# A hybrid decoder layer on one Trainium2 core: expert gathers spread more thinly over the early stages, a later transpose step, and a shorter decode of top-k positions

## The chip, the cores and the metric

The kernel is one launch on one core of one Trainium2 chip. The metric is device time in microseconds (us). Three runs of the kernel before took 3212.78, 3213.16 and 3213.87 us; the median is 3213.16 us. One further execution was profiled: it took 3213.83 us, of which the profile's span covers 3212.0 us.

## The reference, cut to what matters

One layer over 1024 tokens of width 1024, batch 1:

```
h = rms_norm(x);  proj = h @ w_in                    # q, k, v of 4 attention heads; q, k, v, o, i, f of 4 mLSTM heads
da_out = differential attention(q, k, v)             # causal, ALiBi, 4 heads of 2 x 64
ml_out = chunkwise mLSTM(conv(q), conv(k), v, i, f)  # 4 heads of 128
x = x + concat(da_out, ml_out) @ w_out
q = rms_norm(x) @ w_query                            # 8 heads x 2 halves x 128
s = q . sub_keys                                     # 128 keys per half
sv, si = top_k(s, 16)                                # per half
top_s, pos = top_k(sv0[:, None] + sv1[None, :], 16)  # 16 of the 256 pairs
eidx = 128 * si0[row of pos] + si1[column of pos]    # 8 x 16 experts per token
x = x + sum_k softmax(top_s)_k * gelu(h2 . expert_u[eidx_k]) * expert_v[eidx_k]
x = x + sigmoid(rms_norm(x) @ w_ple_gate) * (p @ w_ple_proj)
out = rms_norm(x)
```

There are 16384 experts, each a row of 1024 floats in `expert_u` and in `expert_v`. `h2` is the normalised input of this step.

## The kernel before, in words

**Stages.** The 1024 tokens are two parts of 512 (T); a part is four tiles of 128 tokens. `front(0)` and `front(1)` compute, for one part each, the projections, attention, mLSTM, the output projection, and the retrieval scores with their top 16 per half. Of the eight tiles, the first three (NS = 3, the sparse tiles) fetch their chosen expert rows by gather; the other five (640 tokens) go through all experts densely: `dense_up` multiplies them with all of `expert_u` in 128 blocks `j`, applies GELU and stores the result, and builds the gate matrix that says which token takes which expert; `dense_down` multiplies with all of `expert_v` in 128 blocks, four at a time. `tail` does the last gate, projection and norm for each of the eight tiles, in the order 4, 0, 5, 6, 7, 1, 3, 2. Matmuls run in a split form: each fp32 operand is a high and a low part (`hi` by ACT, `lo` by DVE), and three products replace one.

**The gathered steps.** For the three sparse tiles, `sparse` is a generator of 400 steps: 24 units of 16 experts, and one more unit's worth of steps that finishes the last. A step has a u half and a v half. The u half (line 803) gathers one row of `expert_u` per token (512 KB, an indirect DMA issued by POOL, line 788) and takes its dot product with `h2` on DVE (line 804). The v half, 16 steps later, gathers the row of `expert_v` and adds it, scaled, to the running sum `ya` on DVE (line 822). The first 16 steps have only the u half, the last 16 only the v half. Ahead of them in the same generator stand 14 steps of `topk2` for the first two tiles. When the last v half of a tile is done, the sum is stored to DRAM (line 826), and `tail` reads it back (line 1086).

**What paces them.** `pump(x)` (line 210) adds x to a running sum and emits one step for each whole unit; it is called from `project` (line 289, F_RATE[0], 29 times in `front(1)`), at the eight loads of output weights (line 609, F_RATE[2]), at the 16 query projections (lines 658 and 669, F_RATE[1]), at each block j of `dense_up` (line 940: the first UP_RATE value below block UP_RATE[2], then the second), four times DOWN_RATE per group of four blocks of `dense_down`, and TAIL_RATE twice per tile of `tail`, until the steps are used up. In `front(0)` nothing is pumped (the rates are multiplied by `part`). The program's instructions are put in order at build time by a planner that gives each emitted instruction a priority in order of emission; what `pump` emits comes 800 places later (LAG), so gathers fill gaps that the planner sees on DVE. The DVE half of a step also stands behind the last weight split before it (`behind`, line 203). On the chip each engine takes its instructions strictly in that order.

**Buffers.** Gathered rows land in a ring: `ru` and `rv` have NR = 4 buffers each from `front(1)` to the end of `dense_up`, six each in `dense_down`, two each from group FLUSH of `dense_down` on and in `tail`. In `front` most [128, 512] tiles come from one ring named `t2` with 8 buffers: q and k after projection (lines 370, 379), their copies to both 64-row halves (`doubled`, line 257, four per head in part 0 and six in part 1), and attention and mLSTM temporaries.

**Order of the steps in `front`.** `attention(h)` is a generator of six steps (five for its four query tiles, the sixth with the norm `ro` of the outputs and their transposes, lines 444 to 449), `ml_inputs(h)` of four (each one projection), `mlstm(h)` of four (the fourth with the transposes of its outputs, line 558), `qkv(h)` of three (each one projection). The loop over heads (lines 570 to 580) calls them in turn.

**Decoding.** A top-k position `pos` in the 50 candidate pairs is taken apart in `topk2b` (lines 751 to 762): row a starts at OFFS[a] (0, 16, 24, 29, 33, 36, 38, 40, 42, 43, ... 49) and has COUNTS[a] columns (16, 8, 5, 4, 3, 2, 2, 2, then eight rows of one). For each a from 1 to 15 two instructions add the row's index to `i0`, and two subtract the length of the row before from `bb`, which ends as the column. This runs for four groups of two tiles: one in `front(1)`, three in the first 42 blocks of `dense_up`.

Of the kernel before, what the change touches and what calls it, by code (L numbers as in the profile page):

```python
# [8 lines left out]
F32 = mybir.dt.float32  # L9
F32R = mybir.dt.float32r  # L10
BF16 = mybir.dt.bfloat16
# [4 lines left out]
OP = mybir.AluOpType  # L16
# [3 lines left out]
P = 128  # L20
D = 1024
S = 1024
T = 512
# [5 lines left out]
K = 16  # L29
# [5 lines left out]
COUNTS = [K // (a + 1) for a in range(K)]  # L35
OFFS = [sum(COUNTS[:a]) for a in range(K)]
# [11 lines left out]
LAG = 800  # L48
FLUSH = 108
NPRE = 4  # L50
NR = 4
NR2 = 2
NRD = 6
RD = 2
# [8 lines left out]
T2 = 8  # L63
# [3 lines left out]
TORD = [4, 0, 5, 6, 7, 1, 3, 2]  # L67
TAIL_RATE = 8.0
TKEYS = [(0, q) for q in range(4)] + [(0, -1), (1, -1)] + [(1, q) for q in range(4)]
F_RATE = (2.4, 1.6, 2.0)  # L70
UP_RATE = (1.0, 1.2, 56)
DOWN_RATE = 1.05


# [1 line left out]
def layer(ctx, tc, x, xT, pT, gcols, grows, win, convw, convb, gbias, lams, wout, wq, subk,  # L76
# [3 lines left out]
    def pool(name, bufs=1, **k):  # L80
        if k.get("space") != bass.MemoryType.DRAM:
            k["reuse_waits"] = "tile"
        return tc.tile_pool(name=name, bufs=bufs, **k)

    v, sc, pe, gp, sy = nc.vector, nc.scalar, nc.tensor, nc.gpsimd, nc.sync
# [132 lines left out]
    def front(part, ptk):  # L218
        t0 = part * NT
        with ExitStack() as c1:  # L220
# [4 lines left out]
            with pool(f"pa{part}", bufs=1) as pa:  # L225
# [29 lines left out]
                        sc.activation(kab[halves[c], 1 - c, 1, n * T:(n + 1) * T], kb[halves[c]], AF.Copy)  # L255

                def doubled(src, c):
                    d = pa.tile([P, T], F32, name="t2", bufs=T2)
                    for half in halves:
                        sy.dma_start(d[half], src[halves[c]])  # L260
                    return d
# [44 lines left out]
                for i in range(NT):  # L306
                    v.scalar_tensor_tensor(gt[:, i, :], gps[:, i, 0:8], r1[:, i:i + 1], gb, op0=OP.mult,
                                           op1=OP.add)
# [58 lines left out]

                def qkv(h):
                    ps = project(h * 7 + 0)
                    qT = pa.tile([P, T], F32, name="t2", bufs=T2)  # L370
                    v.scalar_tensor_tensor(qT, ps, DA_SCALE, rb, op0=OP.mult, op1=OP.mult)
                    queries(qT, h)
                    vv = pa.tile([P, S // P, P], F32, name="vv", bufs=1)
                    if part:
                        keys(kt_s[h], 0)
                        sy.dma_start(vv[:, :NT, :], v_s[h])
                    yield
                    ps = project(h * 7 + 1)
                    kT = pa.tile([P, T], F32, name="t2", bufs=T2)
                    v.tensor_tensor(kT, ps, rb, op=OP.mult)  # L380
                    if part < NPART - 1:
                        sy.dma_start(kt_s[h], kT)
                    keys(kT, part)
                    yield
                    ps = project(h * 7 + 2)
                    by_tile(vv[:, t0:t0 + NT, :], token_major(ps), lambda i: r1[:, i:i + 1])
                    if part < NPART - 1:
                        sy.dma_start(v_s[h], vv[:, :NT, :])
                    st["qkv", h] = (qT, kT, vv)
                    yield  # L390
# [171 lines left out]
                def step(*gens):  # L562
                    for g in gens:
                        if g is not None:
                            next(g, None)
# [3 lines left out]
                cell = None  # L569
                for h in range(H):  # L570
                    att, inputs = attention(h), ml_inputs(h)
                    step(att, cell)
                    for _ in range(4):
                        step(inputs, att)
                    step(att)
                    cell = mlstm(h)
                    nxt = qkv(h + 1) if h + 1 < H else None
                    for _ in range(3):
                        step(cell, nxt)
                step(cell)  # L580

                mh = act.tile([P, DC, T], F32R, name="ahi")
# [125 lines left out]
    def topk2b(part, pt_, tgs):  # L708
        sv, sfa = fcs["sv", part]
        t0 = part * NT  # L710
        i0a, i1a = sel_i[part]
        gsa = gsm[part]
        TG = 2
        G = TG * PH
        for tg in tgs:
            def grp(a):
                return a[:, tg:tg + TG, :].rearrange("p t (h k) -> p (t h) k", k=K)

            svf = sv[:, tg:tg + TG].rearrange("p t h c k -> p (t h) c k")
            sif = sfa[:, tg:tg + TG].rearrange("p t h c k -> p (t h) c k")  # L720
            cand = pt_.tile([P, G, NCAND], F32, name="cand")
            for a in range(8):
                n = COUNTS[a]
                behind(v.tensor_tensor(cand[:, :, OFFS[a]:OFFS[a] + n], svf[:, :, 1, 0:n],
                                       svf[:, :, 0, a:a + 1].to_broadcast([P, G, n]), op=OP.add))
            behind(v.tensor_tensor(cand[:, :, OFFS[8]:], svf[:, :, 0, 8:],
                                   svf[:, :, 1, 0:1].to_broadcast([P, G, 8]), op=OP.add))
            yield True
            ts = pt_.tile([P, G, K], F32, name="ts")
            pu_ = pt_.tile([P, G, K], U32, name="pu_")  # L730
            for j in range(G):
                wk = pt_.tile([P, NCAND], F32, name="wk2", bufs=2)
                v.max(out=ts[:, j, 0:8], in_=cand[:, j, :])
                v.max_index(out=pu_[:, j, 0:8], in_max=ts[:, j, 0:8], in_values=cand[:, j, :])
                v.match_replace(out=wk, in_to_replace=ts[:, j, 0:8], in_values=cand[:, j, :],
                                imm_value=NEG)
                v.max(out=ts[:, j, 8:16], in_=wk)
                v.max_index(out=pu_[:, j, 8:16], in_max=ts[:, j, 8:16], in_values=wk)
                if j % 4 == 3:
                    yield True  # L740
            pos = pt_.tile([P, G, K], BF16, name="pos")
            v.tensor_copy(pos, pu_)
            dl = pt_.tile([P, G, 2, K], BF16, name="dl")
            v.tensor_copy(dl[:, :, :, 0:1], sif[:, :, :, 0:1])
            v.tensor_tensor(dl[:, :, :, 1:], sif[:, :, :, 1:], sif[:, :, :, :K - 1], op=OP.subtract)
            i0, i1 = grp(i0a), grp(i1a)
            bb = pt_.tile([P, G, K], BF16, name="bb")
            v.tensor_copy(i0, dl[:, :, 0, 0:1].to_broadcast([P, G, K]))
            v.tensor_copy(i1, dl[:, :, 1, 0:1].to_broadcast([P, G, K]))
            v.tensor_copy(bb, pos)  # L750
            for a in range(1, K):
                tmp = pt_.tile([P, G, K], BF16, name="tmp", bufs=1)
                v.scalar_tensor_tensor(tmp, pos, float(OFFS[a]),
                                       dl[:, :, 0, a:a + 1].to_broadcast([P, G, K]),
                                       op0=OP.is_ge, op1=OP.mult)
                v.tensor_tensor(i0, i0, tmp, op=OP.add)
                tmp = pt_.tile([P, G, K], BF16, name="tmp", bufs=1)
                v.tensor_scalar(tmp, pos, float(OFFS[a]), float(COUNTS[a - 1]), op0=OP.is_ge,
                                op1=OP.mult)
                v.tensor_tensor(bb, bb, tmp, op=OP.subtract)  # L760
                if a % 3 == 0:
                    yield True
            for b in range(1, K):
                tmp = pt_.tile([P, G, K], BF16, name="tmp", bufs=1)
                v.scalar_tensor_tensor(tmp, bb, float(b),
                                       dl[:, :, 1, b:b + 1].to_broadcast([P, G, K]),
                                       op0=OP.is_ge, op1=OP.mult)
                v.tensor_tensor(i1, i1, tmp, op=OP.add)
                if b % 4 == 0:
                    yield True  # L770
            if t0 + tg < NS:
                v.scalar_tensor_tensor(grp(eidx[part]), i0, 128.0, i1, op0=OP.mult, op1=OP.add)
            g_ = grp(gsa)
            gs = pt_.tile([P, G], F32, name="gs")
            v.tensor_tensor(g_, ts, ts[:, :, 0:1].to_broadcast([P, G, K]), op=OP.subtract)
            sc.activation(g_, g_, AF.Exp)
            v.tensor_reduce(out=gs, in_=g_, axis=AX.X, op=OP.add)
            gr = pt_.tile([P, G], F32, name="gr")
            v.reciprocal(gr, gs)
            v.tensor_tensor(g_, g_, gr[:, :, None].to_broadcast([P, G, K]), op=OP.mult)  # L780
            yield True

    ring, stored = {}, set()
# [365 lines left out]
    rstk = ctx.enter_context(ExitStack())  # L1149
    ptk = rstk.enter_context(pool("ptk", side="right"))  # L1150
    fc = fstk.enter_context(pool("fc"))
    front(0, ptk)
    ring["pool"] = rstk.enter_context(pool("rg", side="right"))
    ring["bufs"] = NR
    pumped["gen"] = chain(lambda: topk2(0, ptk, [0]), lambda: sparse(range(NS), rs))
    front(1, ptk)
    fstk.close()
    dense_up(ptk)
    stk.close()
    yap = ctx.enter_context(pool("yap"))  # L1160
# [93 lines left out]
```

## Time and profile before

| | us |
|---|---|
| median of three runs | 3213.16 |
| profiled execution | 3213.83 |
| its span | 3212.0 |
| PE (matmul) busy in the span | 2954.8 (92%) |
| DVE busy | 2521.5 (79%) |
| ACT busy | 1160.2 (36%) |
| POOL busy | 1013.0 (32%) |

Stages in the span, by when their first and last instructions run: `front(0)` to about 460 us, `front(1)` to about 1060, `dense_up` to about 2110, `dense_down` to about 3057, `tail` to the end.

PE is the tensor engine, DVE the vector engine, ACT the scalar engine, POOL the engine that issues gathers, SP the queue of most other DMAs. "L804" is line 804 of the kernel. An arrow such as "ru<-ru,sh" reads output<-inputs by the program's tile names. In square brackets stands how long the engine sat idle before an instruction and what ended the wait.

### The profile page before, as it was taken

What the parts mean: (1) busy time and instruction counts of PE and PEld (TensorE: products, weight loads), DVE (VectorE), ACT (ScalarE), POOL (GpSimd) and SP (SyncE); (2) the same over time, 40 slices, a digit from 0 to 9 for tenths busy, and PEclk for the clock granted to TensorE, in tenths of its full rate; (3) what the DMA queues carried; (4) which work ended last, traced back from release to release, by engine and by line L of the source; (5) the groups of instructions that cost most, each with busy time, mean ns of one, the idle gap of its engine ahead of it and who ended that gap; (6) DMA issues with size and microseconds to landing.
All of it is one profiled execution on the core that took longest, in us unless ns stands there. A gap on an engine that the chain in (4) does not pass through costs nothing.

```text
span 3212.0 us, 44687 instructions
## 1 busy us (share of the span) xinstructions
PE 2954.8 (92%) x16367; PEld 2601.1 (81%) x16367; DVE 2521.5 (79%) x5381; ACT 1160.2 (36%) x1994; POOL 1013.0 (32%) x786
## 2 busy tenths in 40 slices
PE   7998889887579799999999999988989999999987
PEld 6776767676467799999999999977878888887866
DVE  5564689888889999978766667557878888888786
ACT  5664335554322232245343433322222222222233
POOL 0000000344541544412433334343333444442330
PEclk9998989998789899999999999989999999999999
DMA  5333433678874788876888878899989999998762
GB/s 163 96 107 108 143 120 95 232 234 274 323 264 147 290 317 313 284 262 244 329 314 299 293 278 311 313 343 343 327 316 337 334 334 331 334 327 286 265 209 92
DMA packets 317148, 829.53 MB, mean 258 GB/s; under 512 B 26240, under 2 KB 115200, under 8 KB 314368
## 3 DMA queue, kind: packets, MB, share of 16 engines
q0 software_dynamic: 112608, 410.04, 36.2%
q1 hardware_dynamic: 185888, 374.68, 33.8%
q10 hardware_dynamic: 18432, 41.95, 3.5%
q8 instruction: 128, 2.10, 0.3%
q14 instruction: 92, 0.75, 0.1%
HBM read 715.95 MB, written 102.24 MB: 255 GB/s over the span
## 4 chain that ended last, share of the span: by engine, by line
PE 53%; DVE 19%; issue 14%; DMA 8%; POOL 4%; ACT 2%; SPq 0%; POOLq 0%; DVEq 0%; ACTq 0%
PE A L143 16%; PE mm L143 10%; PE keep L143 6%; DVE ya L822 3%; PE S L143 3%; DVE ru L804 2%; DMA rv<-in_ev,eidx 2%; PE Y L135 2%; PE Y L134 2%; PE Y L136 2%; DMA raw<-in_vr 2%; POOL rv L788 2%; PE pg L894 2%; PE pg L895 2%; DVE tlo L842 2%
## 5 line engine op out<-in xcount | busy, mean ns | idle before, releaser
L788 POOL DMA_INDIRECT ru<-in_eu,eidx x384 | 507.5, 1321 | 1201.8 <-DVE ru L804 845.1
L788 POOL DMA_INDIRECT rv<-in_ev,eidx x384 | 497.5, 1296 | 442.6 <-DVE ya L822 300.7
L842 DVE TENSOR_TENSOR tlo<-raw,thi 128x1024 fp32r<-128x1024 f32 x256 | 312.9, 1222 | 299.1 <-issue 168.5
L822 DVE SCALAR_TENSOR_TENSOR ya<-rv,cf,ya 128x1024 f32<-128x1024 f32 x384 | 492.8, 1283 | 40.3 <-DMA rv<-in_ev,eidx 28.1
L841 ACT ACTIVATE thi<-raw 128x1024 fp32r<-128x1024 f32 x256 | 268.0, 1058 | 683.4 <-PE A L143 380.8
L804 DVE SCALAR_TENSOR_TENSOR ru<-ru,sh 128x1024 f32<-128x1024 f32 x384 | 468.8, 1221 | 20.8 <-DMA ru<-in_eu,eidx 19.6
L143 PE MATMUL A<-ahi,thi 128*128 128x384 f32 x1024 | 348.7, 341 | 4.3 <-ACT ga L954 4.3
L143 PE MATMUL A<-alo,thi 128*128 128x384 f32 x1024 | 346.6, 338 | 0.0
L143 PE MATMUL mm<-ahi,whi 128*128 128x512 f32 (+1 forms) x752 | 299.7, 402 | 22.2 <-ACT ahi L234 12.4
L143 PE MATMUL mm<-alo,whi 128*128 128x512 f32 (+1 forms) x752 | 286.2, 393 | 7.1 <-DVE alo L235 7.1
L134 PE MATMUL Y<-thi,ph 128*128 128x512 f32 x640 | 250.3, 391 | 6.6 <-ACT thi L841 4.8
L143 PE MATMUL A<-xh,thi 128*128 128x256 f32 x1024 | 250.8, 283 | 0.7 <-ACT xh L933 0.7
L143 PE MATMUL A<-xl,thi 128*128 128x256 f32 x1024 | 250.6, 282 | 0.1
L135 PE MATMUL Y<-tlo,ph 128*128 128x512 f32 x640 | 249.8, 390 | 0.5 <-DVE tlo L842 0.5
L136 PE MATMUL Y<-thi,pl 128*128 128x512 f32 x640 | 249.5, 390 | 0.0
L143 PE MATMUL A<-ahi,tlo 128*128 128x384 f32 x1024 | 202.7, 338 | 13.8 <-DVE tlo L842 13.7
L1021 ACT ACTIVATE ph<-aq 128x640 fp32r<-128x640 f32 x128 | 87.5, 729 | 330.8 <-PE Y L135 325.3
L143 PEld LDWEIGHTS A<-ahi,thi 128*128 128x128 f32 x1024 | 195.1, 191 | 4.5 <-ACT ga L954 4.5
L143 PE MATMUL mm<-ahi,wlo 128*128 128x512 f32 (+1 forms) x752 | 193.7, 388 | 5.5 <-DVE wlo L194 5.5
L143 PEld LDWEIGHTS A<-xh,thi 128*128 128x128 f32 x1024 | 195.0, 190 | 1.0 <-ACT xh L933 0.9
L143 PEld LDWEIGHTS A<-xl,thi 128*128 128x128 f32 x1024 | 194.8, 190 | 0.3 <-DVE xl L934 0.3
L143 PEld LDWEIGHTS A<-alo,thi 128*128 128x128 f32 x1024 | 195.0, 190 | 0.0
(462 smaller groups left out, 6160.0 us busy)
## 6 DMA issues: line engine op xcount, KB each, us to landing
raw<-in_ut SPq DMA_DIRECT2D x128, 512.0 KB, 5.9
raw<-in_vr SPq DMA_DIRECT2D x128, 512.0 KB, 5.5
ga_s<-ga ACTq DMA_DIRECT2D x128, 320.0 KB, 5.6
g_s<-st SPq DMA_DIRECT2D x20, 2048.0 KB, 8.3
gq<-g_s SPq DMA_DIRECT2D x32, 1280.0 KB, 10.8
aq<-ga_s SPq DMA_DIRECT2D x32, 1280.0 KB, 8.7
wraw<-in_win SPq DMA_DIRECT2D x58, 512.0 KB, 3.4
wraw<-in_wq SPq DMA_DIRECT2D x32, 512.0 KB, 3.7
```

The costliest lines, as they stand in the source:

```text
L134: pe.matmul(o, lh, rh, start=start, stop=False)
L135: pe.matmul(o, lh, rl, start=False, stop=False)
L136: pe.matmul(o, ll, rh, start=False, stop=stop)
L143: pe.matmul(o, ll if p == "l" else lh, rl if p == "r" else rh, start=start and p == "h", stop=stop and n == last and p == names[-1])
L788: gp.indirect_dma_start(out=b, out_offset=None, in_=table, in_offset=bass.IndirectOffsetOnAxis(ap=eidx[part][:, i, k:k + 1], axis=0))
L804: behind(v.scalar_tensor_tensor(b, b, 1.0, st["h", tl], op0=OP.mult, op1=OP.mult, accum_out=st["d", n][:, j:j + 1]))
L822: op = v.scalar_tensor_tensor(ya, b, st["c", n][:, j:j + 1], ya, op0=OP.mult, op1=OP.add)
L841: sc.activation(hi, raw, AF.Copy)
L842: anchor(v.tensor_sub(lo, raw, hi.bitcast(F32)))
L894: pe.matmul(pg[:, b, :], o0[:, a, :, b], w0[:, a, :, b], start=True, stop=False)
L895: pe.matmul(pg[:, b, :], o0[:, a, :, b], w1[:, a, :, b], start=False, stop=True)
L1021: sc.activation(ph, av, AF.Copy)
```

## The change

- Rates of the gathered steps: F_RATE, UP_RATE.
- The gather ring: 3 buffers each in `front(1)` (NR), a new pool `rgu` with 4 each (NRU) opened for `dense_up`.
- `doubled` takes its copies from a ring `dd` of its own with 2 buffers, and q and k after projection from a ring `qk` with 2; `t2` keeps 8.
- In the loop over heads the fourth step of the head before's mLSTM comes after the first projection of `ml_inputs` (it came before it). The last line calls the attention generator twice; as it has six steps, of which five are taken above, the second call finds it ended.
- Decoding: for a from 9 to 15 nothing is subtracted from `bb`; at a = 8 one instruction sets `bb` to zero where `pos` is at least OFFS[8] = 42. The instructions for `i0` stay.

```diff
-NR = 4
+NR = 3
+NRU = 4
+NDD = 2
-F_RATE = (2.4, 1.6, 2.0)
-UP_RATE = (1.0, 1.2, 56)
+F_RATE = (1.8, 1.3, 1.5)
+UP_RATE = (0.9, 1.45, 40)
...
                 def doubled(src, c):
-                    d = pa.tile([P, T], F32, name="t2", bufs=T2)
+                    d = pa.tile([P, T], F32, name="dd", bufs=NDD)
...
-                    qT = pa.tile([P, T], F32, name="t2", bufs=T2)
+                    qT = pa.tile([P, T], F32, name="qk", bufs=2)
...
-                    kT = pa.tile([P, T], F32, name="t2", bufs=T2)
+                    kT = pa.tile([P, T], F32, name="qk", bufs=2)
...
                     att, inputs = attention(h), ml_inputs(h)
-                    step(att, cell)
-                    for _ in range(4):
+                    step(att)
+                    step(inputs, cell, att)
+                    for _ in range(3):
                         step(inputs, att)
-                    step(att)
                     cell = mlstm(h)
                     nxt = qkv(h + 1) if h + 1 < H else None
-                    for _ in range(3):
-                        step(cell, nxt)
+                    step(att, cell, nxt, cell, nxt, att, cell, nxt)
                 step(cell)
...
-                tmp = pt_.tile([P, G, K], BF16, name="tmp", bufs=1)
-                v.tensor_scalar(tmp, pos, float(OFFS[a]), float(COUNTS[a - 1]), op0=OP.is_ge,
-                                op1=OP.mult)
-                v.tensor_tensor(bb, bb, tmp, op=OP.subtract)
+                if a < 8:
+                    tmp = pt_.tile([P, G, K], BF16, name="tmp", bufs=1)
+                    v.tensor_scalar(tmp, pos, float(OFFS[a]), float(COUNTS[a - 1]), op0=OP.is_ge,
+                                    op1=OP.mult)
+                    v.tensor_tensor(bb, bb, tmp, op=OP.subtract)
+                elif a == 8:
+                    v.scalar_tensor_tensor(bb, pos, float(OFFS[8]), bb, op0=OP.is_lt, op1=OP.mult)
...
-    ring["pool"] = rstk.enter_context(pool("rg", side="right"))
+    fring = ExitStack()
+    ring["pool"] = fring.enter_context(pool("rg", side="right"))
     ring["bufs"] = NR
...
     fstk.close()
+    fring.close()
+    ring["pool"] = rstk.enter_context(pool("rgu", side="right"))
+    ring["bufs"] = NRU
     dense_up(ptk)
```

## Rows read from the trace of the kernel before

**Rows 1.** Busy time of each engine by stretch: PE, PEld, DVE, ACT, POOL, PE clock, DMA share, GB/s.

```profile
680.00:772.00 92.00, 72.30 (x375) 59.28 (x376) 82.67 (x158) 45.56 (x104) 46.15 (x38) 0.87 0.80 272
...
1043.00:1080.00 37.00, 19.24 (x88) 16.25 (x88) 37.00 (x163) 5.14 (x8) 18.93 (x14) 0.72 0.68 229
...
1500.00:2097.00 597.00, 596.72 (x4233) 592.83 (x4232) 413.44 (x454) 232.61 (x321) 236.37 (x176) 1.00 0.85 304
...
2125.00:2250.00 125.00, 102.21 (x434) 83.66 (x434) 89.55 (x114) 28.34 (x37) 51.10 (x42) 0.90 1.02 359
...
2400.00:2650.00 250.00, 250.00 (x1105) 207.01 (x1104) 212.40 (x270) 60.69 (x75) 100.75 (x76) 1.00 0.96 334
...
3060.00:3156.00 96.00, 84.49 (x360) 66.36 (x361) 75.38 (x192) 35.93 (x68) 27.78 (x23) 0.95 0.61 198
```

**Rows 2.** Line 804 on DVE by stretch: busy (two records per u half), clock, DMA.

```profile
460.00:870.00 410.00, 74.74 (x122) 0.86 0.68 228
...
717.00:749.00 32.00, 13.42 (x22) 0.79 0.98 368
870.00:940.00 70.00, 18.43 (x30) 0.88 0.85 317
1043.00:1080.00 37.00, 8.59 (x14) 0.72 0.68 229
```

**Rows 3.** Line 822 on DVE by stretch: busy (one record per v half).

```profile
717.00:749.00 32.00, 14.06 (x11) 0.79 0.98 368
...
1500.00:2097.00 597.00, 113.10 (x88) 1.00 0.85 304
3060.00:3156.00 96.00, 26.94 (x21) 0.95 0.61 198
```

**Rows 4.** DVE in order of time: start, duration, line, operation, tiles.

```profile
721.22 0.20 DVE L116 TENSOR_SCALAR ro_m<-oss 128x4 f32<-128x4 f32 x1
...
730.16 1.27 DVE L822 SCALAR_TENSOR_TENSOR ya<-rv,cf,ya 128x1024 f32<-128x1024 f32 x1
731.36 0.15 DVE L125 SCALAR_TENSOR_TENSOR ro_u<-ro_h,ro_u 128x4 f32<-128x4 f32 x1
731.43 1.22 DVE L804 SCALAR_TENSOR_TENSOR ru<-ru,sh 128x1024 f32<-128x1024 f32 x1
...
732.57 0.15 DVE L123 TENSOR_TENSOR ro_h<-ro_u 128x4 f32<-128x4 f32 x1
...
735.26 0.16 DVE L125 SCALAR_TENSOR_TENSOR ro_u<-ro_h,ro_u 128x4 f32<-128x4 f32 x1
```

**Rows 5.** PE in order of time, the transposes of lines 448 and 558.

```profile
735.91 1.06 PE L448 MATMUL tr<-ident,t 128*128 128x128 f32 x3 [12.17 <-ACT t L364]
...
589.90 0.33 PE L558 MATMUL tr<-ident,t 128*128 128x128 f32 x1 [0.26 <-ACT t L364]
```

**Rows 6.** Who waited for whom: PE from 870 to 940, then 1030 to 1085.

```profile
PE tr L635 <- DVE dg L631: 17.3, 1, 17.3
...
PE A L143 <- DVE tlo L842: 13.7, 1, 13.7
```

**Rows 7.** The chain that ended last, DMA pieces between 720 and 770.

```profile
726.62 7.47 DMA ru<-in_eu,eidx
...
749.45 9.97 DMA t<-kt_s
```

**Rows 8.** Groups of instructions by line: decode of positions; busy, mean ns.

```profile
L760 DVE TENSOR_TENSOR bb<-bb,tmp 128x256 bf16<-128x256 bf16 x60 | 17.4, 291 | 0.7
...
L758 DVE TENSOR_SCALAR tmp<-pos 128x256 bf16<-128x256 bf16 x60 | 13.8, 230 | 0.8
```

**Rows 9.** Who waited for whom: DVE from 3060 to 3156.

```profile
DVE ya L822 <- DMA rv<-in_ev,eidx: 15.3, 10, 3.2
DVE ru L804 <- DMA ru<-in_eu,eidx: 5.0, 2, 2.7
```

**Rows 10.** The chain that ended last, from 3030 on: the last v half.

```profile
3154.38 1.28 DVE ya L822
```

## Prediction

> **What bounds the kernel now.** I read the table of busy time by stretch first, because the bound changes from stage to stage. In `dense_up` and in the middle of `dense_down` PE is busy without a gap (596.72 of 597 us, 250.00 of 250) while DVE has 20 to 30% to spare [rows 1]: work put there on DVE or DMA costs nothing until it makes PE wait. `front(1)` is different. In a head's period of 92 us (680 to 772) PE works 72.3 and DVE 82.7 [rows 1], and none of them is full: they wait for each other in turn. At the end of `front(1)` (1043 to 1080) DVE is full and PE half idle. In the tail (3060 to 3156) DVE works 75.4 of 96 us, and its waits for gathered rows, 15.3 + 5.0, fill the rest [rows 1, 9]: there DVE sets the pace.
>
> The order of time on DVE shows what it does in `front(1)`. The norm of an attention head's output is a chain of dependent operations of about 0.07 us each in the queue; between its first at 721.22 and its last, which ends at 735.4, gathered steps stand in the queue, so that a chain of about 2 us takes 14 [rows 4]. PE waits 12.17 us for it [rows 5]. From 717 to 749 eleven steps run, 22 records of u halves and 11 of v halves [rows 2, 3]. The norm before the retrieval has the same form: PE waits 17.3 us for it [rows 6]. And at 1064 the first table split of `dense_up` comes behind gathers and top-k work: PE waits 13.7 us [rows 6].
>
> What a step costs on DVE is the distance of starts: a v half 1.20 us (730.16 to 731.36), a u half 1.14 (731.43 to 732.57) [rows 4], together 2.34.
>
> **How many steps move.** In `front(1)` 29 projections, 8 output weights and 16 query weights pump 29 x 2.4 + 8 x 2.0 + 16 x 1.6 = 111.2 steps before, 29 x 1.8 + 8 x 1.5 + 16 x 1.3 = 85.0 after: 26.2 fewer. In `dense_up` 56 x 1.0 + 72 x 1.2 = 142.4 become 36 + 88 x 1.45 = 163.6: 21.2 more. `dense_down` keeps 134.4. Of the 414 steps, 26 are left for the tail before, 31 after: five more.
>
> Do the gaps in `front(1)` fill from a stock, so that a lower rate only empties it? Up to 870, 122 / 2 = 61 u halves have run [rows 2]; the 29 projections supply 69.6 - 14 = 55.6, so the queue already draws on steps of the output weights. Supply is the limit, and fewer steps means fewer in the queue.
>
> **Part by part.** Each term against the profiled execution, 3213.8 us (span 3212.0 and 1.8 around it; 0.7 over the median of the runs shown).
>
> 1. The bursts at four head ends: 11 steps become 11 x 0.75 = 8.25, so 2.75 x 2.34 = 6.4 us less each, where PE stands idle for 12. The other 1.45 steps of a head's 4.2 (3.4 us) stand beside PE work; I count 1. Sum 4 x 7.4 = -30. Bounds -39 (4 x 4.2 x 2.34) and -10 (the last burst has no projection behind it, and the planner may put others' work there).
> 2. Output projection: four steps fewer, 9.4 us at most; fifteen u halves run there [rows 2], about a third ahead of the norm, beside PE. I take -6, bounds -9 and 0.
> 3. Query stage: 4.8 steps fewer; seven run between 1043 and 1080 [rows 2], of which I take away 1.7: -4, bounds -11 and 0.
> 4. Decoding: seven pairs of 0.230 + 0.291 us go and at a = 8 two instructions become one: 3.7 us of DVE a group, 15 in all [rows 8]; the new one's own duration is not in the trace with this comparison, so 0.2 to 0.5. Three groups lie beside PE-bound `dense_up` and are worth nothing; if PE waited there, 11. The one in `front(1)`: -1, bounds -4 and 0.
> 5. The ring of three: a row lands 7.47 us after its issue [rows 7]; with 1.14 or 1.20 for its use a buffer serves one step in about 9 us; three give one per 3.0 us, four one per 2.25. The bursts run at 32 / 11 = 2.9. I take +2 a burst, +8, bounds 0 and +15 (every step at 3.0 or more).
> 6. `dd` with two buffers: the copies of the stored keys, which land 9.97 us after issue [rows 7], were queued right behind the queries' copies; they now wait on SP until those are converted, with weight loads queued behind them on SP. Four us later for three heads would be +12; lighter gather traffic and PE's two projections in between take back most. I take +3, bounds -6 and +16. In part 0 the four copies of a head are not close in time: 0. The opposite effect, that `t2` with fewer users frees earlier, I leave in the bound.
> 7. The transposes: only the mLSTM's fourth step moves, behind one projection of 24 matmuls. PE waited 0.26 us there [rows 5], the norm is off the path, and its store of the result goes out later behind a weight load on SP, read only at the end. -1 for both parts, bounds -2 and +3. The attention step does not move: its sixth call stands where it stood, and the added call does nothing.
> 8. `dense_up`: from 1500 to 2097, 88 steps ran in 597 us [rows 3]; at 1.45 they become 106, 43 us more DVE, 413 -> 456 of 597. PE covers it. Four steps fewer ahead of block 40, beside the late top-k work: -2. Bounds -4 and +15 (below). The new pool's first buffers overlap the old ring's; only gathers wait for that.
> 9. Into `dense_down`: 2125 to 2250 is full of DMA (1.02, 359 GB/s) and PE loses 23 of 125 us [rows 1]. A stock larger by two or three steps of 1.05 MB is 6 to 8 us of transfer, mostly in rows not yet needed: +2, bounds 0 and +8.
> 10. The tail: five more steps on DVE. 21 v halves took 96 us [rows 3], 4.6 each, DVE full or waiting. The least is 5 x 2.34 = 11.7, the most 5 x 4.4 = 22 (two buffers, a row 7 us away). After the last v half, which ends at 3155.7 [rows 10], 56 us remain, in which part of it can be made up: +13.
>
> `front(0)` and `front(1)`: -30 - 6 - 4 - 1 + 8 + 3 - 1 = -31. Rest: -2 + 2 + 13 = +13. Sum -18: 3213.8 - 18 = 3196.
>
> **A rule weighed.** The stretch at 359 GB/s loses PE time, the one at 334 GB/s and a share of 0.96 loses none [rows 1]. The Trainium skill ("DMA: Bandwidth & Descriptors", Specifications) gives a core about 358 GB/s of HBM when its neighbour streams as well. The trace agrees: no long stretch is above 359. By that rule alone `dense_up` would have room to about 358 and term 8 would stay at nothing; it would not tell at what load a table comes late, which is the rival's question.
>
> **Rivals.**
>
> *Every step taken out of `front(1)` pays in full* (it is a serial chain through DVE): 26.2 x 2.34 = 61 us, rings free, rest +13: 3166. For it: DVE is at 90% of a head's period. Against: PE's 72 of 92 us are near its own limit, and a third of the steps run beside PE.
>
> *Nothing*: the bursts shrink by half as much (-15), ring and `dd` take 15, terms 2 to 4 give 8, the tail costs 15: +7 to -3, about 3214. For it: the ring of three is just at the pace of the bursts. Against: supply falls by a quarter whatever the ring does.
>
> *Slower: DMA in `dense_up`.* Now 304 GB/s and a share of 0.85 [rows 1]; 18 steps of 1.05 MB more in 597 us are +32 GB/s: 336 and 0.94. If tables then land late, PE loses some part of what it lost at 359 (18%). At a third of that, 6% over the 715 us from block 40 on, it is +43: 3239. It decides from 18 us lost on, 2.5% of that stretch, where the forecast's gain is gone; above 24 the kernel is measurably slower. Against: at 334 and 0.96 PE lost nothing, and `dense_up` has three table buffers.
>
> *It does not do what it says*: the attention transposes are not moved. This is so by the code; it costs nothing against the forecast, which counts it at zero.
>
> **How the numbers follow.** What a measurement can tell from no change is 0.2%, 6.4 us. The forecast (3178 to 3207) 0.50; full payment (below 3178) 0.20; nothing (3207 to 3220) 0.14; slower (above 3220) 0.16, by DMA or by terms 5, 6 and 10 all at their upper bounds. Faster 0.70, same 0.14, slower 0.16. For 8 in 10 the range leaves out a little of the full payment and most of the slower case: 3163 to 3221.
>
> **What would show it.** Steps 1 and 2: PE's waits for the attention output's norm fall from 12 to about 6 us a head, the 17.3 us wait to about 11, a head's period from 92 to about 85. Step 5: DVE waits for `ru` and `rv` rows in the bursts. Step 6: PE waits at line 411. Step 8: PE stays at 100% from 1500 on, DVE near 76%, DMA near 0.94. Step 10: 26 v halves after `dense_down` instead of 21, and the tail longer by 10 us or more. Wrong would be: head periods unchanged; PE gaps at the table splits of `dense_up`; a tail that does not grow.

## The result, and the profile after

The kernel after takes 3191.2 us in the median of its runs (3181.6 to 3192.6), the kernel before beside it 3213.4; the ratio is 0.9922, 95% interval 0.9906 to 0.9939. The profiled execution has a span of 3190.8 us, 21.2 less than that of before. The forecast was 3196.

By stage, from the start of the last row of matmuls of each in both traces (the last transposes of the mLSTM, those of the retrieval norm, the last query product, the last block of `dense_up`, the last `Y`, the end of the span), against the terms of the forecast that fall there. The first two columns are points in time, the last two are changes, all in us:

| stage ends with | before | after | this stage | forecast |
|---|---|---|---|---|
| heads (and `front(0)`) | 857.2 | 830.1 | -27.1 | -21 (terms 1, 4 to 7) |
| output projection | 926.4 | 895.3 | -4.0 | -6 |
| query stage | 1047.6 | 1016.4 | 0.0 | -4 |
| `dense_up` | 2132.9 | 2113.3 | +11.5 | -2 |
| `dense_down` | 3056.4 | 3034.4 | -2.4 | +2 |
| tail | 3212.0 | 3190.8 | +0.7 | +13 |

The front's -31 came as forecast, though the heads gave 6 more than their terms and the two stages behind them 6 less; the rest is 10 against 13, but as two errors of 12 to 14 that cancel. The page shows DVE with 5321 instructions, 60 fewer than the 5381 of before, 15 for each of the four groups that are decoded:

```profile
PE 2954.2 (93%) x16367; PEld 2599.5 (81%) x16367; DVE 2512.5 (79%) x5321; ACT 1159.0 (36%) x1992; POOL 1021.9 (32%) x786
```

First the busy time of the kernel after, by stretch, with the columns of [rows 1]; the first three lines are the periods of the heads in `front(1)`.

```profile
557.40:639.20 81.80, 70.52 (x375) 58.12 (x375) 67.34 (x161) 45.23 (x106) 26.17 (x23) 0.90 0.65 213
639.20:731.40 92.20, 70.82 (x376) 59.86 (x376) 77.02 (x151) 50.10 (x113) 40.10 (x29) 0.85 0.75 244
731.40:808.30 76.90, 62.30 (x351) 51.78 (x351) 60.46 (x127) 40.65 (x98) 28.16 (x23) 0.92 0.61 198
...
1470.00:1670.00 200.00, 188.28 (x1331) 186.55 (x1329) 163.00 (x186) 76.82 (x104) 111.54 (x81) 0.97 0.92 352
1670.00:2070.00 400.00, 400.00 (x2837) 397.69 (x2836) 295.89 (x331) 154.43 (x216) 187.50 (x140) 1.00 0.89 330
```

The periods are 81.8, 92.2 and 76.9 us; before they were these, from the same points:

```profile
559.20:643.70 84.50, 67.91 (x375) 56.29 (x375) 72.13 (x174) 45.67 (x106) 30.56 (x25) 0.91 0.69 232
643.70:735.90 92.20, 72.24 (x375) 59.09 (x375) 81.67 (x158) 46.40 (x107) 45.03 (x35) 0.87 0.76 252
735.90:828.10 92.20, 67.19 (x352) 54.90 (x352) 81.68 (x156) 45.28 (x106) 45.94 (x38) 0.85 0.80 264
```

POOL's count, mostly gathers, fell from 35 to 29 in the second period and from 38 to 23 in the third: the heads are not thinned alike. The second has lost 4.7 us of DVE's work and nothing of its length; the third lost 21 and 15. These are PE's rows at the transposes behind the norms of the attention outputs, the first and the third of before (the second, 12.17, is in [rows 5]):

```profile
643.72 1.06 PE L448 MATMUL tr<-ident,t 128*128 128x128 f32 x3 [15.13 <-ACT t L364]
...
828.07 1.06 PE L448 MATMUL tr<-ident,t 128*128 128x128 f32 x3 [16.21 <-ACT t L364]
```

And these are all three after, then the retrieval norm and the first table ([rows 6] before):

```profile
639.24 1.06 PE L450 MATMUL tr<-ident,t 128*128 128x128 f32 x3 [8.24 <-ACT t L366]
...
731.37 1.06 PE L450 MATMUL tr<-ident,t 128*128 128x128 f32 x3 [15.38 <-ACT t L366]
...
808.30 1.06 PE L450 MATMUL tr<-ident,t 128*128 128x128 f32 x3 [10.17 <-ACT t L366]
...
895.25 4.89 PE L636 MATMUL tr<-dg,xg 128*128 128x128 f32 x24 [13.96 <-DVE dg L632]
...
1031.43 0.69 PE L145 MATMUL A<-ahi,thi 128*128 128x384 f32 x1 [13.84 <-ACT thi L845]
```

The second norm is waited for longer than before, and its chain on DVE is longer too (16.1 us from its first to its last operation; 14.2 before). The gathered halves in it fell from 14.1 to 10.2 us of DVE's time. What came in is the conversion of the next head's q, from the new rings `qk` and `dd`, with a wait for ACT in the middle of the norm:

```profile
725.67 0.69 DVE L279 TENSOR_TENSOR qab<-dd,qab 64x512 fp32r<-64x512 f32 x1 [3.69 <-ACT qab L277]
```

In `dense_up`, once its first blocks are past, PE idles once for more than 0.3 us, at the third of five gate tiles (the tiles of 128 tokens whose gate matrix is built; the first two are begun together, and the expectations below call this one the second), for `w`:

```profile
1534.88 0.52 PE L898 MATMUL pg<-w,o 128*128 128x128 f16 x3 [11.43 <-DVE w L889]
```

DVE's order there, one line per operation (start, duration, what it waited for): the gate tile's indices `pt` were ready at 1516.7; their copy `it`, from which `o` and `w` follow, stands behind eight gathered halves and a table split, ahead of which and between which DVE waited for rows.

```profile
1506.65 1.29 DVE L826 SCALAR_TENSOR_TENSOR ya<-rv,cf,ya 128x1024 f32<-128x1024 f32 x1 [4.18 <-DMA rv<-in_ev,eidx]
...
1516.13 1.23 DVE L808 SCALAR_TENSOR_TENSOR ru<-ru,sh 128x1024 f32<-128x1024 f32 x1 [1.74 <-DMA sh<-h_s]
...
1527.19 1.28 DVE L826 SCALAR_TENSOR_TENSOR ya<-rv,cf,ya 128x1024 f32<-128x1024 f32 x1 [1.63 <-DMA rv<-in_ev,eidx]
1528.40 0.55 DVE L872 CAST it<-pt 128x384 f16<-128x384 f32 x1
...
1533.61 1.22 DVE L889 TENSOR_TENSOR w<-o,it 128x2048 f16<-128x2048 f16 x1
```

### The profile page after: what moved, and what is told of

The parts are those of the page before. It is cut to its first block, busy times and chain, and to the rows that moved or that the text cites. A ratio compares the mean times of both kernels' runs of the same rounds, so it can differ in the third digit from the quotient of the medians.

```text
span 3190.8 us, 44623 instructions
## 1 busy us (share of the span) xinstructions
PE 2954.2 (93%) x16367; PEld 2599.5 (81%) x16367; DVE 2512.5 (79%) x5321; ACT 1159.0 (36%) x1992; POOL 1021.9 (32%) x786
## 4 chain that ended last, share of the span: by engine, by line
PE 29%; DMA 7%; DVE 7%; issue 7%; POOL 1%; ACT 1%; DVEq 0%; SPq 0%; POOLq 0%; ACTq 0%
PE A L145 13%; PE keep L145 6%; DMA raw<-in_vr 3%; DMA rv<-in_ev,eidx 2%; PE Y L137 2%; PE Y L136 2%; PE Y L138 2%; DVE ya L826 2%; PE pg L898 1%; PE pg L899 1%; DMA ru<-in_eu,eidx 1%; DVE tlo L846 1%; DVE ru L808 1%; DVE aq L1024 1%; DVE yac L1045 1%
## 5 line engine op out<-in xcount | busy, mean ns | idle before, releaser
L792 POOL DMA_INDIRECT ru<-in_eu,eidx x384 | 499.5, 1301 | 1165.4 <-DVE ru L808 857.0
L792 POOL DMA_INDIRECT rv<-in_ev,eidx x384 | 514.4, 1340 | 465.7 <-DVE ya L826 321.1
L145 PE MATMUL A<-ahi,thi 128*128 128x384 f32 x1024 | 349.5, 341 | 14.1 <-ACT thi L845 13.8
L145 PE MATMUL mm<-ahi,whi 128*128 128x512 f32 (+1 forms) x752 | 300.0, 403 | 21.2 <-ACT ahi L236 12.8
L1025 ACT ACTIVATE ph<-aq 128x640 fp32r<-128x640 f32 x128 | 87.4, 728 | 338.1 <-PE Y L137 332.9
```

The costliest lines, as they stand in the source:

```text
L145: pe.matmul(o, ll if p == "l" else lh, rl if p == "r" else rh, start=start and p == "h", stop=stop and n == last and p == names[-1])
L792: gp.indirect_dma_start(out=b, out_offset=None, in_=table, in_offset=bass.IndirectOffsetOnAxis(ap=eidx[part][:, i, k:k + 1], axis=0))
L1025: sc.activation(ph, av, AF.Copy)
```

## The experiments

All ratios are to the kernel before on the same chip, with 95% intervals; 0.001 is 3.2 us. One execution can stand 10 us from the median (3181.6 beside 3191.2): a second profile of the kernel after (run 11) has 32 us less in the heads instead of 27 and 5.9 more in `dense_up` instead of 11.5; runs 4 and 6, whose `front` is that of the kernel after, have 22 and 19 less in the heads. So stages are read from several traces.

**1. The rates alone.**

```diff
 (the kernel before)
-F_RATE = (2.4, 1.6, 2.0)
-UP_RATE = (1.0, 1.2, 56)
+F_RATE = (1.8, 1.3, 1.5)
+UP_RATE = (0.9, 1.45, 40)
```

> The kernel before with the two new rates and nothing else. Theory A (fewer steps in the queue make the whole gain; the rings are nearly free): front(1) gives back 28 to 31 us, the tile switch and its 11 us wait in dense_up come as in the kernel after, so 3188 to 3196 us. Rival B (the separate rings for the copied queries and keys make about half of the gain): 3203 us or more. Rival C (the rings cost what terms 5 and 6 say, 11 us together, and the rates gain 42): 3178 to 3184 us.

3183.4 us, 0.9919 (0.9905 to 0.9934). The whole gain is there without rings, order or decoding. The retrieval norm comes at 891.6, 34.7 us earlier than before. The median misses A's range by 5 us and lies at the upper edge of C's, but C's 42 us for the rates is not in the trace. So A's main point stands: fewer steps make the whole gain. Its other point, rings that are nearly free, is tested by the next runs. The periods are 84.5, 87.4 and 78.2 us. The second norm, with 10.2 us of gathered halves as in the kernel after, is waited for 5 us less than there, and no `qab` waits within it:

```profile
730.85 1.06 PE L448 MATMUL tr<-ident,t 128*128 128x128 f32 x3 [10.15 <-ACT t L364]
```

So what the second head did not gain is not the rates' doing.

**2. All but the rates.**

```diff
 (the kernel after)
-F_RATE = (1.8, 1.3, 1.5)
-UP_RATE = (0.9, 1.45, 40)
+F_RATE = (2.4, 1.6, 2.0)
+UP_RATE = (1.0, 1.2, 56)
```

> The kernel after with both old rates: rings, order and decoding as changed. Theory A: 3208 to 3214 us (order and decoding 1 to 2 us each, rings nothing). Rival B (rings make half of the gain): about 3198 us. Rival C (rings cost 11 us): 3220 to 3224 us.

3221.1 us, 1.0030 (1.0017 to 1.0044): about 10 us slower, which is rival C's time. At the old rates the rings are not free, and A falls there. DVE's waits for gathered rows from 700 to 945, first before, then in this run (total, times, longest):

```profile
DVE ru L804 <- DMA ru<-in_eu,eidx: 2.1, 3, 1.1
...
DVE ya L822 <- DMA rv<-in_ev,eidx: 0.5, 1, 0.5
```

```profile
DVE ru L808 <- DMA ru<-in_eu,eidx: 8.4, 5, 4.4
...
DVE ya L826 <- DMA rv<-in_ev,eidx: 5.4, 8, 2.1
```

From 2.6 to 13.8 us; the retrieval norm is 12.2 us late.

**5. The ring of three alone.**

```diff
 (the kernel before)
-NR = 4
+NR = 3
+NRU = 4
 (and the pool rgu for dense_up, as in the change)
```

> The kernel before with the gather ring of three in front(1) and four again from dense_up on; rates, t2, order and decoding as before. Theory A2 (at the old rates the ring of three is what made the run without the new rates 12 us later at the retrieval norm; with t2 shared as before nothing else changes): DVE waits 10 us or more for gathered rows between 700 and 940, front(1) ends 8 to 12 us later, ratio to before 1.002 to 1.004. Rival F (it was the two-buffer rings for copies and projections): DVE's waits for rows stay near 3 us and the ratio is 0.999 to 1.001.

3219.3 us, 1.0028 (1.0015 to 1.0041), and the same waits, 7.9 + 4.9 us:

```profile
DVE ru L805 <- DMA ru<-in_eu,eidx: 7.9, 12, 2.6
...
DVE ya L823 <- DMA rv<-in_ev,eidx: 4.9, 7, 1.4
```

A2 holds, F falls: the ring of three costs 9 us at the old rates, and `dd`, `qk`, order and decoding together nothing that can be measured in the whole time (run 2 less run 5). In the heads they do move time about, as the part on terms 1 and 5 shows. In the kernel after, from 700 to 900, the waits for rows are 0.9 + 1.9 us: with fewer steps three buffers nearly suffice.

**3. The old order.**

```diff
 (the kernel after)
-                    step(att)
-                    step(inputs, cell, att)
-                    for _ in range(3):
+                    step(att, cell)
+                    for _ in range(4):
                         step(inputs, att)
+                    step(att)
                     cell = mlstm(h)
                     nxt = qkv(h + 1) if h + 1 < H else None
-                    step(att, cell, nxt, cell, nxt, att, cell, nxt)
+                    for _ in range(3):
+                        step(cell, nxt)
```

> The kernel after with the old order of the loop over heads. Theory A (the moved mLSTM step is worth 1 us, term 7): 3191 to 3194 us. Rival D (the moved step, not the smaller bursts, is why heads 2 to 4 got 23 us shorter): the head periods go back to 92 and the time to 3205 us or more.

3187.9 us, 0.9935 (0.9917 to 0.9954), head periods 83.4, 87.1 and 78.2. D falls; the move is worth nothing that can be measured, and A's time (3191 to 3194) was missed by 3 us, less than the scatter.

**11. The kernel after once more.**

> The kernel after, unchanged, on the chip of these runs, for a comparison within one call: ratio to before 0.990 to 0.994. With the rates-only run at 0.992 this would leave the ring of three, the separate rings, the order and the decoding together within 6 us of nothing at the new rates.

3187.1 us, 0.9930 (0.9915 to 0.9944). Beside 0.9919 for the rates alone, all the rest of the change costs 1 to 4 us, within the intervals nothing. The wait for `w` is there again, 12.3 us.

**4. Gate blocks four blocks of `j` later.**

```diff
 (the kernel after)
-GST = 14
+GST = 18
```

> The kernel after with the gate blocks of dense_up begun four blocks of j later (GST 18 for 14); steps and rates as after. Theory A (the 11.4 us PE wait is a coincidence in time: the gathers' change of tile stalls DVE's queue just where a gate tile's short chain of pt, it, o and w is due): the wait is gone, 3179 to 3183 us. Rival E (the higher rate alone makes the gate chain late): a wait of about 11 us stays at the second gate tile or another, 3189 to 3193 us.

3191.5 us, 0.9939 (0.9924 to 0.9954): no gain. The time is E's, the wait is neither theory's: 5.2 us for `w`, and 4.1 for a table came in.

**7. Still fewer steps in `front(1)`.**

```diff
 (the kernel before)
-F_RATE = (2.4, 1.6, 2.0)
-UP_RATE = (1.0, 1.2, 56)
+F_RATE = (1.4, 1.3, 1.5)
+UP_RATE = (0.9, 1.58, 40)
```

> The kernel before with rates still lower in front(1) and higher in dense_up (F_RATE 1.4, 1.3, 1.5; UP_RATE 0.9, 1.58 from block 40): 11.6 further steps leave front(1), as many steps as in the kernel after are left for the tail, and the gathers' change of tile falls at block 61 instead of 54. By the rates-only run a step out of front(1) is worth 1.3 us: -15 there. Theory A (the wait at the second gate tile is a coincidence with the change of tile): it is gone, together 3158 to 3166 us. Rival E (the rate in dense_up makes the gate chain late): the wait is 11 us or more, together 3167 to 3180 us. If DMA in dense_up is full at the higher rate: 3185 us or more.

3161.0 us, 0.9844 (0.983 to 0.9857). The time is A's, the reason is not: PE waits 20.6 us for `w` in three places. The first, 10.9 us up to 1493, lies 30 us ahead of the gathers' change to the next sparse tile (1523), so that the change of tile is not its cause. Of the second, 4.9 us at 1620, it is: just ahead of the operations that make `w`, DVE stood 14.9 us for the new tile's running sum.

```profile
1616.10 1.28 DVE L822 SCALAR_TENSOR_TENSOR ya<-rv,cf,ya 128x1024 f32<-128x1024 f32 x1 [14.86 <-DMA ya<-x_s]
```

The time comes from the heads:

```profile
558.30:628.10 69.80, 67.88 (x375) 56.23 (x375) 63.15 (x158) 44.05 (x104) 22.09 (x19) 0.98 0.64 215
628.10:700.00 71.90, 68.25 (x375) 55.86 (x376) 56.81 (x125) 46.42 (x107) 18.02 (x13) 0.98 0.59 184
700.00:774.90 74.90, 63.25 (x352) 52.09 (x352) 66.06 (x134) 42.59 (x103) 26.57 (x22) 0.97 0.70 220
```

PE is now busy 84 to 97% of a period, the granted clock is 0.97 to 0.98 instead of 0.85 to 0.92, and PE's waits for the norms are 0.57, 0.33 and 6.49 us. A period is 17 us shorter than before for 29 / 4 x 1.0 = 7.25 steps: 2.4 us a step, the full price, where 1.3 was expected. In run 1 it was 6.3 us for 4.35 steps, 1.4 each.

**6. Ten more steps for the tail.**

```diff
 (the kernel after)
-DOWN_RATE = 1.05
+DOWN_RATE = 0.97
```

> The kernel after with DOWN_RATE 0.97 for 1.05: ten more steps are left for the tail (41 instead of 31). Theory S (five more steps cost nothing because the last v half ended 57 us before the end before and 37 us after, and that slack is now used up or nearly): the lane of v halves ends 40 us later and the end follows by 25 to 40, dense_down gains 0 to 5, so 3211 to 3229 us. Rival G (the tail's v halves lie beside PE work and cost about 0.2 us each): 3188 to 3194 us.

3241.6 us, 1.0090 (1.0076 to 1.0105): 50 us above the kernel after, more than S said, and G falls. PE's wait for tile 2's sum, read back from DRAM, first after, then here:

```profile
3162.61 1.97 PE L1105 MATMUL tr<-ident,x 128*128 128x128 f32 x8 [2.34 <-DMA x<-x_s]
```

```profile
3211.89 1.97 PE L1105 MATMUL tr<-ident,x 128*128 128x128 f32 x8 [53.97 <-DMA x<-x_s]
```

The last v half starts at 3204.7 instead of 3153.5; in both kernels some 37 us follow it. Before it was 57. The five steps of the change used up 20 us that were free; each of the next ten costs 5.

**8 and 12. More DMA in `dense_up`, old rates.**

```diff
 (the kernel before; run 8, then run 12 in its place)
                 sc.dma_start(ga_s[j], ga)
+                sc.dma_start(dx_s[j], ut[j][:, 0:512])
...
+                sc.dma_start(dx_s[j], ga)
```

> The kernel before with one further transfer for each block j of dense_up: 256 KB of expert_u's transpose copied to a scratch array in DRAM that nobody reads; steps, rates, order and engines' work as before. Theory H (the 11 us wait of PE for w in dense_up comes from DMA load: at 350 GB/s and more rows land late, DVE waits for them in its queue, and the gate's short chain stands behind): in the 200 us stretches between 1500 and 2100 DMA rises from about 300 to 330 to 360 GB/s, PE waits 5 us or more for w or for a table, 3215 to 3235 us. Rival I (it is the number of steps queued on DVE, whatever the DMA load): no such wait over 2 us, 3206 to 3214 us.

3225.1 us, 1.0037 (1.0024 to 1.0051), and inconclusive: nothing ties the copy to its block, and all 128 were issued from 0.8 to 270 us. They made `front(0)` 9.4 us longer; from 1500 to 2097 DMA moves 303 GB/s, before 304.

> The kernel before with a second store of each activated block ga (320 KB, to a scratch array that nobody reads), so that the further traffic falls into dense_up itself; steps, rates, order and engines' work as before. Theory H (DMA load makes the gate's chain late): DMA in 1460 to 2060 rises from about 300 to 335 to 355 GB/s, and PE waits 5 us or more for w, as in the kernels with the higher rates; 3216 to 3235 us. Rival I (the load alone does not do it; it needs many gathered halves packed into the one stretch at the second gate tile): PE's waits for w stay under 2 us in all and dense_up is as long as before, 3206 to 3216 us.

3230.5 us, 1.0064 (1.005 to 1.0077). The load is where it should be, at the lower end of what H asked for, and PE waits 0.28 us for `w`, as before:

```profile
1460.00:1660.00 200.00, 200.00 (x1442) 196.34 (x1441) 154.33 (x165) 89.98 (x116) 71.99 (x54) 1.00 0.88 334
1660.00:1860.00 200.00, 199.72 (x1422) 198.26 (x1421) 137.24 (x151) 79.27 (x108) 74.34 (x57) 1.00 0.93 339
1860.00:2060.00 200.00, 200.00 (x1421) 198.63 (x1420) 135.61 (x147) 79.37 (x109) 74.58 (x57) 1.00 0.92 333
```

H falls at this load for that wait. The price is elsewhere: `dense_up` is 7.5 us longer, by late activations and splits, and the first product of `dense_down` waits 16.1 us for its table, before 5.3. The load did not reach the 352 GB/s of after's worst stretch, though by its share (0.93 against 0.92) it did. What differs there is the packing. v halves (line 822 or its like) in 52 us about the third gate tile: length, DVE busy (count), clock, DMA share, GB/s; before, after, in run 4 and in run 12:

```profile
1498.00:1550.00 52.00, 12.90 (x10) 1.00 0.93 354
```

```profile
1476.00:1528.00 52.00, 17.59 (x14) 0.99 0.93 356
```

```profile
1504.00:1556.00 52.00, 16.78 (x13) 0.97 0.96 376
```

```profile
1498.00:1550.00 52.00, 12.90 (x10) 1.00 0.87 339
```

Ten steps pass without PE waiting, with the further store too; with thirteen PE waited 5.2 us for `w` (and 4.1 for a table), with fourteen 11.4. DVE is busy 39.8 of the 52 us before and 39.5 after, so it is not out of time; but of what is left it spends 12.3 us waiting for gathered rows and the new tile's activations after, 1.5 before and 5.6 in run 12. Counted in the same way ahead of the copy `it` at every gate tile of the kernels with a higher rate, thirteen or fourteen v halves stand at each wait for `w` of 4.8 to 12.7 us but the one above that the running sum explains, and twelve or fewer where PE waits at most 0.3 us.

In the 56 us ahead of that stretch before and after have two v halves each: while the first two gate tiles fill DVE's order, few gathers stand in it, and what is due comes in one burst, at a rate that the rows do not follow. Run 4 had ten ahead of its thirteen, so the pause is not needed for the wait. That the burst is the cause is argued, not shown: it fits all kernels with either rate, but a kernel with the rates of after and another packing alone was not run.

**9 and 10. Towards a better version.**

```diff
 (the kernel before; run 9, then run 10 in its place)
+F_RATE = (1.4, 1.3, 1.5)
+UP_RATE = (1.2, 1.45, 40)
...
+F_RATE = (1.4, 1.0, 1.0)
+UP_RATE = (1.25, 1.525, 40)
```

> The rates of the run with 11.6 further steps out of front(1), but with dense_up's steps spread more evenly (1.2 before block 40, 1.45 from there; the same 175 in all). Theory H: no 200 us stretch from 1260 to 2060 above 345 GB/s, PE's waits for w fall from 20.6 to 6 us or less, 3144 to 3156 us. Rival I (the steps' DVE time delays the gate chain wherever they stand): waits of 15 us or more, 3157 to 3166 us.

> As the spread run, with 8.8 further steps moved from the output projection and the query stage to dense_up (F_RATE 1.4, 1.0, 1.0; UP_RATE 1.25, 1.525). If a step out of these stages is worth 1.3 us as those out of the heads were: 11 less than the spread run, 3133 to 3147 us. If dense_up is full by DMA at this rate: as the spread run or later, 3146 to 3165 us.

3158.6 us, 0.9829 (0.9815 to 0.9842), the time of rival I, and 3147.3 us, 0.9804 (0.9788 to 0.9820), where the two cases meet. Both beat the kernel after; run 10 by some 40 us, with the old rings, order and decoding. An even rate did not spread the burst: run 9 still has 360 GB/s from 1460 to 1660 and waits 11.2 us for `w`, which is neither H's 6 nor I's 15; run 10 waits 10.2. Run 10's 11 us over run 9 are the expected sum, but not from the query stage: from the retrieval norm to the last query product it takes 121.2 us at a rate of 1.0 and 121.2 at 1.6. In the two traces the heads, whose rate is the same, give 4.4 of it and `dense_down` 2.8; that the moved steps made it is not shown.

## Why the prediction was right, and where it was not

**Terms 1 and 5, heads.** The mechanism was right in kind: gathered halves stand among the short operations that PE waits for, and fewer of them make the heads shorter; run 7, with waits of 0.57, 0.33 and 6.49 us, shows it plainly. I put terms 1 and 5 to 7 at -20; the trace gives some -25 in `front(1)` before the output projection. The rates alone give 28.5 less `front(0)`'s 1, so term 1's -30 was nearly exact in its sum. That is in part luck, for the place that it named gave a third of it. PE's waits for the three norms were to fall by 6 each; they went from 43.5 to 33.8 in all after, and with the rates alone to 35.1 (total, times, longest):

```profile
PE tr L448 <- ACT t L364: 35.1, 3, 15.3
```

The rest of run 1's gain came where term 1 did not look: the waits at the mLSTM's last transposes (11.8 to 7.0) and for its state `nst` (7.4 to nothing), and PE's own work, done in some 6 us less at a higher clock.

The norms one by one are not all the rates' either. Over nine traces the waits are these, in us; run 3 has the rings but the old order of steps, and no run has them so at the old rates:

| | first | second | third |
|---|---|---|---|
| before, run 5: old rates, old `t2` | 15.1, 13.5 | 12.2, 14.9 | 16.2, 16.0 |
| run 1: new rates, old `t2` | 15.3 | 10.2 | 9.6 |
| run 2: old rates, rings `dd` and `qk` | 8.0 | 15.4 | 15.5 |
| after, runs 11, 4, 6: new rates, rings | 7.8 to 9.3 | 15.4 to 16.0 | 10.0 to 10.6 |
| run 3: as after, old order | 11.6 | 13.9 | 8.6 |

The third wait falls with the rates. The first falls and the second rises with the rings and the order, whatever the rate; in each of the six traces with the rings DVE waits 2.0 to 3.9 us for `qab` within the second norm, in the others not at all. The sum hides it.

The failing step is in term 5: I charged the ring +2 for each of four bursts at the old pace of 2.9 us a step, after term 1 had thinned those bursts. At the old rates +8 would have been right (9 measured, run 5); at the new ones it is at most 1 to 4, with all other terms in it. Not foreseen is the distribution: 3, 0, 15 and 7 us for the four heads in the first trace after, by the rates alone 0, 5, 14 and 9. "6.4 less each" was a mean.

**Term 2**: -4.0 in the trace (-6.3 with the rates alone) for -6; PE's wait for that norm fell from 17.3 to 14.0, where about 11 was expected. **Term 3**: 0 for -4. PE's wait at the first table is 13.8 us as before [rows 6], and the stage has the same length at three rates: what stands in DVE's queue there delays nothing that ends the stage.

**Terms 4, 6 and 7**: forecast at 1, 3 and 1 us; together nothing that can be measured. Term 6's sign did not come: PE's waits for the converted keys (line 411, 413 after) fell from 7.2 to 2.0 us. The later copies showed in another place, the wait for `qab` within the second head's norm. The attention transposes are not moved: their place after is that of before.

**Term 8** failed: -2 forecast, +5.9 and +11.5 in two executions. I had the mean right (330 GB/s for 336, no idle PE from 1670 on), and concluded from the mean over 600 us that PE covers it. The one stretch of 50 us with a burst was already at 354 GB/s before, and with four steps more there PE waited 11 us. Before had lost 4.3 us to a late activated block at 1294, which after did not; so the stage grew by less than the new wait in one of the two executions. The rival that charged DMA in `dense_up` 43 us named the place, but PE lost 6% of one 200 us stretch (188.28 busy) and nothing of the rest.

**Term 9**: -2.4 for +2, within its scatter. **Term 10** failed: +0.7 for +13. The count was right (22 v halves after 3058 before, 27 after 3036 after), and so was the price of a step on DVE's lane: 4 to 5 us. What I put aside as "part of it can be made up" was all of it: 20 of the 57 us after the last v half were slack. Run 6 shows its end.

**Rivals.** Full payment did not happen at these rates (34.7 us for 26.2 steps in run 1, 1.3 each), but for the next 11.6 it did, and more: run 7's heads end 32 us before run 1's, 2.8 a step. The price followed PE's waits and clock more than DVE's share.

**The rule weighed.** The failing step of term 8 hung on no ceiling, but the ceiling was wrong as well: I read 359 GB/s in [rows 1] as the most that a long stretch moves. Run 10 moved 377 for 200 us. The Trainium skill gives about 358 GB/s as the limit of one core, half of its HBM stack ("DMA: Bandwidth & Descriptors", Specifications), and says that a core streaming alone measures well above that share ("HBM Reference", Specifications (TRN2)). This kernel runs on one core, and run 10's trace agrees that 358 is no ceiling here, by 5%:

```profile
1460.00:1660.00 200.00, 189.78 (x1338) 188.45 (x1337) 162.09 (x186) 72.99 (x103) 116.68 (x85) 0.97 0.97 377
```

## What to carry to other kernels

Price work that is moved into an engine's free time in the stretch where it lands, here at its densest 50 us, and not by the stage's mean. When two edits act on the same burst, price the second against what the first leaves. Check the place that a term names, and not its sum alone: here a sum came out while the named waits gave a third of it. And look for slack behind the last link of a lane before charging it: it is free up to an edge (31 steps here) and costs the full lane price beyond.

## What the runs showed of the hardware

Where PE's waits for the norms went (run 7), its mean granted clock rose (1.00 is the level of 2.4 GHz, 0.50 that of 1.2): 0.85 to 0.92 in the heads of before and after, 0.97 to 0.98 in run 7, so that PE's own busy time fell too (72.2 to 68.3 us in the second period). And in run 8 the copies without a tie to their block were issued from the start of the program: 128 of them in the first 270 us. In run 10 one core moved 377 GB/s over 200 us.
